# Six more places for first-stage weights, scale and shift in one run, and banks taken two by two

## The chip, the cores and the metric

The kernel runs on one core of one Trainium2 chip. Its time is device microseconds from launch to end, given as the median of several executions. Besides, one execution was profiled; durations and waits below are from that one. Its engines are called as in the profile: PE is TensorE, PEld its weight loads, DVE is VectorE, ACT ScalarE, POOL GpSimd, and SP SyncE, which issues most transfers.

## What is computed

Two layers on a stream of 256 tokens with 2048 channels, beside 256 tokens of context, all in 32-bit floats:

```python
shift, scale, gate = split(silu(c) @ ada_w[i] + ada_b[i], 3)
h  = rms_norm(x, norm_g[i]) * (1 + scale) + shift          # the same for ctx with c_ctx
# layer 0, heads side by side
p  = h @ w_in                     # query, gate, z, key, value, x, B, C, dt
ya = neighbourhood_attention(q, k, v, k_ctx, v_ctx, rpb) * silu(gate_a)
yb = gated_group_rmsnorm(bidirectional_ssd(conv(x, B, C), dt) + d * x, z)
x  = x + gate * (concat(ya, yb) @ w_out)
# layer 1
bg, cg, hv, g = split(h @ sc_in, 4)
x  = x + gate * ((silu(g) * bg * conv3(cg * hv)) @ sc_out)
```

Scale and shift of layer 0 are needed before anything else: 2 x 2048 columns of `ada_w[0]`, of 2048 rows each. They are wanted for two conditioning vectors, that of the latent tokens and that of the context.

## The kernel before

**Numbers in two parts.** Every wide product is split: a weight block of 128 x 1024 floats lands in a raw place, ScalarE casts it to the rounded type as its high part (L407), VectorE subtracts to get the low part (L414), and TensorE makes three products of high and low parts. There are `NW` = 3 places for high and low parts, taken in turn: block k goes to place k mod 3, and it may be split when fewer than three blocks are ahead of it that aren't used up (`splits_try`, L440; `used`, L463).

**Raw places.** The pool `free_r` has five raw places of 128 x 1024 floats. In the first stage four tiles that are needed later only (`PT0`, `PT1`, `xtm`, `yi`) are lent to it as `spare`, nine in all. SyncE loads blocks in the order of the list `loads` (`issue`, L359) whenever a place is free. When the list of the first stage is through, `later_loads` (L485) takes the lent places out of the pool.

**The order is written by a planner.** The program is straight-line. While it is emitted, `Plan` (L38) keeps a model of when each engine and each piece of a tile is ready, with costs written by hand, and with transfers at `RATE` bytes per ns. Tasks are generators; `pump` (L272) and `force` (L293) emit the next step of a task where the model says that its engine and its inputs are ready. On the chip each engine works its queue strictly in the order emitted, and semaphores hold it where an input isn't there. The model knows a tile in units of 128 columns (L55). The tables `small` and `const` come in two loads each, an early one and a late one (L341, L343; L514, L515).

**The first stage** covers layer 0's key, value and query of the first four heads, and B of the first group, for eight indices j of 256 channels each. Normalised tokens are transposed in four blocks of 128 tokens (two latent, two context). For each j, `ada_gen` (L692) computes scale and shift of its 256 channels: eight raw blocks, four for scale and four for shift (`part` 0 and 1), each against 128 x 32 columns of the conditioning vectors (`cpad`), then a copy by ScalarE (L714), two transposes by TensorE, a sum by VectorE (L722) and two or one small operations. With it, ScalarE and VectorE make the high and low parts of h (L744, L746, L750). Then TensorE does key and value for four token blocks, query for two, and B. Key and value accumulate over j in SBUF: each j's product goes to a bank of its own, and `part_gen` (L770) adds it to the sum (L776). Query and B stay in two banks each over all j. For j = 0 the token blocks come one after the other: the three weight blocks of key, value and query are held until the last token block is through, and then three calls of `used` give their places back (L886).

**The output projection of layer 0** (L1704) runs in three passes over the 16 pairs of `mix` blocks: the first pass makes two groups of 512 output columns, the others one. Each group has two banks for its two token blocks. The first pass comes behind the value projection of the last four heads, whose four banks are copied out by `v_gen` (L998).

## Time and profile before

| | |
|---|---|
| median of 3 runs | 1796.73 us (1795.94 to 1799.53) |
| profiled execution | 1797.29 us |
| its span | 1795.5 us |
| TensorE busy | 1765.5 us, 98% |
| its weight loads | 1490.7 us, 83% |
| VectorE, ScalarE busy | 1292.8 us, 72%; 786.9 us, 44% |
| transfers | 374.67 MB, mean 209 GB/s |
| granted clock | 1.00 |

The span runs from the first to the last instruction of the profiled execution; its time holds 1.8 us around it. In a row of a timeline stand start, duration, engine, line, operation, tiles, shape, the count of instructions that were merged, and in brackets the engine's idle time before it and what ended that. A row of a table of stretches has the stretch, its length, each engine's busy time with its instructions, the granted clock, the transfers' share and GB/s. A row of waits has who waited for what: us in total, times, and the longest.

Matmuls overlap in time on TensorE. So a busy share near 100% doesn't say that nothing is lost, and the distance from one start to the next says more than a duration.

### The profile page before, as it was taken

The numbers are of one execution on the slowest core, as the hardware profiler recorded it, in microseconds if no ns is written. First come the engines' busy times: TensorE is split into PE (matmuls) and PEld (weight loads), VectorE is DVE, ScalarE is ACT, GpSimd is POOL, SyncE is SP. The second block draws the span as 40 slices with busy tenths as digits, with TensorE's granted clock in tenths as the row PEclk, the third lists the DMA queues.
The fourth block names the chain that finished last, engine by engine and source line by source line (L and its number), as shares of the span: only waits on it lengthen the run. The fifth ranks groups of instructions, "written<-read, shape, count | busy, mean of one in ns | idle before, by whom it ended". The sixth has DMA issues, their size and how long they took to land. (4 is left out here: it accounts for less than half of the span.)

```text
span 1795.5 us, 26501 instructions
## 1 busy us (share of the span) xinstructions
PE 1765.5 (98%) x10039; PEld 1490.7 (83%) x10039; DVE 1292.8 (72%) x2073; ACT 786.9 (44%) x1386; POOL 32.5 (2%) x28
## 2 busy tenths in 40 slices
PE   6999999999999999999999999999999999999998
PEld 4677988879888889888888898788888888888887
DVE  5656787888676878676877688786667877565665
ACT  5323544455242445242435344555444444444442
POOL 0000100001000000000001000000000000000000
PEclk9999999999999999999999999999999999999999
DMA  9987744666746665745764567657766786666564
GB/s 359 339 285 239 225 143 125 204 183 200 235 127 202 211 185 175 232 139 173 218 200 134 165 185 247 202 186 268 274 222 225 249 265 222 185 185 187 186 213 150
DMA packets 222368, 374.67 MB, mean 209 GB/s; under 512 B 32432, under 2 KB 69136, under 8 KB 222240
## 3 DMA queue, kind: packets, MB, share of 16 engines
q1 hardware_dynamic: 214928, 366.38, 64.0%
q10 hardware_dynamic: 7312, 6.61, 1.1%
q8 instruction: 78, 1.28, 0.3%
q14 instruction: 50, 0.41, 0.1%
HBM read 367.52 MB, written 6.72 MB: 208 GB/s over the span
## 5 line engine op out<-in xcount | busy, mean ns | idle before, releaser
L407 ACT CAST wH<-raw 128x1024 fp32r<-128x1024 f32 (+1 forms) x439 | 457.8, 1044 | 687.3 <-PE bank L189 561.3
L414 DVE TENSOR_TENSOR wL<-raw,wH 128x1024 fp32r<-128x1024 f32 (+1 forms) x439 | 531.5, 1214 | 250.0 <-ACT wH L407 247.2
L189 PE MATMUL bank<-h,wH 128*128 128x512 f32 x1024 | 362.5, 399 | 1.4 <-DVE h L1669 0.9
L189 PE MATMUL bank<-hH,wH 128*128 128x256 f32 (+1 forms) x1040 | 343.3, 330 | 0.8 <-ACT wH L407 0.8
L189 PE MATMUL bank<-hL,wH 128*128 128x256 f32 (+1 forms) x1040 | 338.0, 325 | 0.0
L189 PE MATMUL bank<-hH,wL 128*128 128x256 f32 (+1 forms) x1024 | 330.8, 323 | 0.8 <-DVE wL L414 0.6
L189 PE MATMUL bank<-h,wL 128*128 128x256 f32 x1024 | 287.6, 281 | 0.0
L189 PE MATMUL bank<-wH,hH 128*128 128x512 f32 x640 | 257.1, 402 | 3.9 <-ACT hH L744 2.6
L189 PE MATMUL bank<-wL,hH 128*128 128x512 f32 x640 | 250.4, 392 | 0.0
L189 PE MATMUL bank<-wH,hL 128*128 128x512 f32 x640 | 249.8, 391 | 0.1
L804 DVE SCALAR_TENSOR_TENSOR acc<-raw,csil,acc 128x512 f32<-128x512 f32 x256 | 191.8, 749 | 63.2 <-DMA raw<-in_ada_w 54.3
L189 PEld LDWEIGHTS bank<-h,wH 128*128 128x128 f32 x1024 | 192.4, 188 | 50.4 <-issue 1.5
L189 PEld LDWEIGHTS bank<-hH,wH 128*128 128x128 f32 x1040 | 196.5, 189 | 18.6 <-ACT wH L407 1.3
L189 PEld LDWEIGHTS bank<-hL,wH 128*128 128x128 f32 x1040 | 196.8, 189 | 15.5
L189 PEld LDWEIGHTS bank<-hH,wL 128*128 128x128 f32 x1024 | 194.0, 189 | 18.3 <-DVE wL L414 1.6
L189 PEld LDWEIGHTS bank<-h,wL 128*128 128x128 f32 x1024 | 193.4, 189 | 0.0
L189 PE MATMUL bank<-wH,mix 128*128 128x512 f32 x512 | 163.1, 393 | 1.1 <-DVE Vt L998 1.1
L189 PEld LDWEIGHTS bank<-wH,hH 128*128 128x128 f32 x640 | 120.2, 188 | 33.8 <-issue 5.0
L189 PEld LDWEIGHTS bank<-wH,hL 128*128 128x128 f32 x640 | 120.2, 188 | 26.1 <-DVE hL L750 0.6
L189 PEld LDWEIGHTS bank<-wL,hH 128*128 128x128 f32 x640 | 120.2, 188 | 24.7 <-DVE wL L430 0.5
L189 PEld LDWEIGHTS bank<-wH,mix 128*128 128x128 f32 x512 | 96.1, 188 | 21.7 <-DVE Vt L998 1.6
L189 PE MATMUL bank<-wL,mix 128*128 128x512 f32 x256 | 100.0, 391 | 0.3 <-DVE wL L414 0.3
(262 smaller groups left out, 1764.0 us busy)
## 6 DMA issues: line engine op xcount, KB each, us to landing
raw<-in_w_in SPq DMA_DIRECT2D x208, 512.0 KB
raw<-in_ada_w SPq DMA_DIRECT2D x128, 512.0 KB
raw<-in_sc_in SPq DMA_DIRECT2D x128, 512.0 KB
raw<-in_w_out SPq DMA_DIRECT2D x64, 512.0 KB
raw<-in_ada SPq DMA_DIRECT2D x37, 512.0 KB
raw<-in_sc_out SPq DMA_DIRECT2D x32, 512.0 KB
tmp<-dram_csr SPq DMA_DIRECT2D x32, 256.0 KB
PT<-in_ada SPq DMA_DIRECT2D x14, 512.0 KB
```

The source lines that it names most:

```text
L189: E(T.matmul(o, l, r, start=start, stop=stop, skip_group_check=True))
L407: E(S.copy(H, v))
L414: E(V.tensor_tensor(out=Lo, in0=v, in1=H.bitcast(F32), op=ALU.subtract))
L804: E(V.scalar_tensor_tensor(out=acc, in0=v[:, j], scalar=csil[:, 2 * k + j:2 * k + j + 1], in1=acc, op0=ALU.mult, op1=ALU.add))
```

## The change

Five things are changed.

1. Six more raw places in the first stage: `KT`, `KL`, `QT` and `QL` (tiles for key and query, two places in each of the first two) are made as tiles of the first stage first, and as what they were only after it. The pool has fifteen.
2. For j from 2 on, `ada_gen` waits for all eight raw blocks and multiplies them in one run into one bank, scale in its first 256 columns and shift in the others; one copy, four transposes, one sum, and three small operations follow. For j = 0 and 1 it stays as it was.
3. High and low parts have a list of free places in the place of k mod 3. At j = 0, when query is through (before the third token block's products), query's place is given back.
4. The planner's `RATE` goes from 270 to 310, and it knows `small` and `const` in units of two columns.
5. The output projection takes two banks ahead of each group's first block, not all banks of a pass ahead of its first block.

```diff
-    RATE = 270.0
+    RATE = 310.0
...
-            return [(n, u) for u in range(lo // 128, hi // 128 + 1)]
+            g = 2 if n[:5] in ("small", "const") else 128
+            return [(n, u) for u in range(lo // g, hi // g + 1)]
...
-    KT, QT, Vt, gt = st([128, 4, 512], "KT", F32R), st([128, 4, 256], "QT", F32R), st([128, 4, 512], "Vt"), st([128, 4, 256], "gt")
-    KL, QL = st([128, 4, 512], "KL", F32R), st([128, 4, 256], "QL", F32R)
+    Vt, gt = st([128, 4, 512], "Vt"), st([128, 4, 256], "gt")
...
-    spare = [t.rearrange("p a b -> p (a b)") for t in (PT[0], PT[1], xtm, yi)]
+    spare = [t.rearrange("p a b -> p (a b)") for t in (PT[0], PT[1], xtm, yi)] + \
+        [st([128, 1024], n, name=f"first{n}") for n in ("QT", "QL")]
+    for n in ("KT", "KL"):
+        kt = st([128, 2, 1024], n, name=f"first{n}")
+        spare += [kt[:, 0], kt[:, 1]]
...
+    free_w, in_use = deque(range(NW)), deque()
+
+    def place():
+        in_use.append(free_w.popleft())
+        return in_use[-1]
...
     def split():
...
+        w = place()
...
-        H = WH[k % NW][:, :nb * n].rearrange("p (b c) -> p b c", b=nb)
-        Lo = WL[k % NW][:, :nb * n].rearrange("p (b c) -> p b c", b=nb)
+        H = WH[w][:, :nb * n].rearrange("p (b c) -> p b c", b=nb)
+        Lo = WL[w][:, :nb * n].rearrange("p (b c) -> p b c", b=nb)
...
-        while pos["split"] < pos["use"] + NW and pos["split"] in RAW:
+        while free_w and pos["split"] in RAW:
...
     def used():
         pos["use"] += 1
+        w = in_use.popleft()
+        if w is not None:
+            free_w.append(w)
         splits_try()
...
+            if j > 1:
+                ks = [("ada", j, part, q) for part in range(2) for q in range(4)]
+                yield when(lambda: all(k in RAW for k in ks))
+                yield W_("PE", *[RAW[k][1] for k in ks], nb=1)
+                ps = bank()
+                for _, _, part, q in ks:
+                    raw, v = RAW.pop(("ada", j, part, q))
+                    for g in range(4):
+                        mm(ps[32 * g:32 * g + 32, part * 256:part * 256 + 256], cpad[:, 4 * q + g, :], v[:, g, :],
+                           q == 0 and part == 0, q == 3)
+                    give_raw(raw)
+                    issue()
+                yield W_("ACT", ps)
+                Rt = tmp()
+                E(S.copy(Rt, ps))
+                yield W_("PE", Rt)
+                for b in range(4):
+                    turn(ps[:, b * 128:(b + 1) * 128], Rt[:, b * 128:(b + 1) * 128])
+                give(free_t, Rt)
+                yield W_("DVE", ps)
+                E(V.tensor_reduce(out=AS, in_=ps.rearrange("p (b g c) -> p b c g", b=4, c=32)[:, :, 0:2, :], axis=AX.X, op=ALU.add))
+                E(V.tensor_tensor(out=A0[:, k2, :], in0=AS[:, 0:2], in1=bc(bs1[:, k2]), op=ALU.add))
+                E(V.tensor_tensor(out=A0[:, k2, :], in0=A0[:, k2, :], in1=bc(g0[:, k2]), op=ALU.mult))
+                E(V.tensor_tensor(out=S0[:, k2, :], in0=AS[:, 2:4], in1=bc(P_("ab0")[:, k2]), op=ALU.add))
+                give(free_b, ps)
+            else:
...
             for t in range(2, 4):
                 force(lambda: ("h", j, t) in got, (urgent,))
+                if t == 2:
+                    free_w.append(in_use[2])
+                    in_use[2] = None
+                    splits_try()
...
     force(lambda: all(("part", 7, key, t) in got for key in "KV" for t in range(4)), (urgent,))
+    KT, QT, KL, QL = st([128, 4, 512], "KT", F32R), st([128, 4, 256], "QT", F32R), st([128, 4, 512], "KL", F32R), st([128, 4, 256], "QL", F32R)
...
     for ns in ((0, 512), (1024,), (1536,)):
-        pss = [banks(2) for n in ns]
+        pss = []
...
-            for ps in pss:
+            for k in range(len(ns)):
+                if ip == 0:
+                    pss.append(banks(2))
+                ps = pss[k]
                 chunk(2 * order[ip], "act", ps, ip == 0, ip == 15, lambda i: (mH[i][:, 0], mH[i][:, 1]))
```

More of the change, by code (lines that the diff above doesn't have):

```diff
@@ L396, in split @@
                 low_part()
-            W = WH[k % NW].rearrange("p (b c) -> p b c", b=nb)
+            W = WH[w].rearrange("p (b c) -> p b c", b=nb)
             E(S.copy(W[:, :, :64], v))
@@ L432, in rest @@
                 RAW.pop(0)
+                place()
                 HL[0] = (H, Lo)
@@ L689 @@
     S0 = st([128, KB, 2], "S0")
+    AS = st([128, 4, 2], "AS")
     g0 = P_("g0")
@@ L695, in ada_gen @@
             k2 = slice(2 * j, 2 * j + 2)
-            for part, dst in ((0, A0), (1, S0)):
-                ps = None
-                for q in range(4):
-                    key = ("ada", j, part, q)
-                    w_ = 2 if j == 0 else 4
-                    if q % w_ == 0:
-                        ks = [("ada", j, part, q + i) for i in range(w_)]
-                        yield when(lambda: all(k in RAW for k in ks))
-                        yield W_("PE", *[RAW[k][1] for k in ks], nb=0 if ps is not None else 1)
-                    if ps is None:
-                        ps = bank()
-                    raw, v = RAW.pop(key)
+            if j > 1:
[5 more added lines that the diff above has]
+                    raw, v = RAW.pop(("ada", j, part, q))
                     for g in range(4):
-                        mm(ps[32 * g:32 * g + 32, :256], cpad[:, 4 * q + g, :], v[:, g, :], q == 0, q == 3)
+                        mm(ps[32 * g:32 * g + 32, part * 256:part * 256 + 256], cpad[:, 4 * q + g, :], v[:, g, :],
+                           q == 0 and part == 0, q == 3)
                     give_raw(raw)
@@ L712, in ada_gen @@
                 yield W_("ACT", ps)
-                Rt = half()
-                E(S.copy(Rt, ps[:, :256]))
+                Rt = tmp()
+                E(S.copy(Rt, ps))
                 yield W_("PE", Rt)
-                for b in range(2):
-                    turn(ps[:, 256 + b * 128:384 + b * 128], Rt[:, b * 128:(b + 1) * 128])
-                give(free_h, Rt)
+                for b in range(4):
+                    turn(ps[:, b * 128:(b + 1) * 128], Rt[:, b * 128:(b + 1) * 128])
+                give(free_t, Rt)
@@ L720, in ada_gen @@
                 yield W_("DVE", ps)
-                p2 = dst[:, k2, :]
-                E(V.tensor_reduce(out=p2, in_=ps[:, 256:].rearrange("p (b g c) -> p b c g", b=2, c=32)[:, :, 0:2, :],
-                                  axis=AX.X, op=ALU.add))
-                if part == 0:
-                    E(V.tensor_tensor(out=dst[:, k2, :], in0=p2, in1=bc(bs1[:, k2]), op=ALU.add))
-                    E(V.tensor_tensor(out=dst[:, k2, :], in0=dst[:, k2, :], in1=bc(g0[:, k2]), op=ALU.mult))
-                else:
-                    E(V.tensor_tensor(out=dst[:, k2, :], in0=p2, in1=bc(P_("ab0")[:, k2]), op=ALU.add))
@@ L729, in ada_gen @@
-                give(free_b, ps)
+                E(V.tensor_reduce(out=AS, in_=ps.rearrange("p (b g c) -> p b c g", b=4, c=32)[:, :, 0:2, :], axis=AX.X, op=ALU.add))
+                E(V.tensor_tensor(out=A0[:, k2, :], in0=AS[:, 0:2], in1=bc(bs1[:, k2]), op=ALU.add))
+                E(V.tensor_tensor(out=A0[:, k2, :], in0=A0[:, k2, :], in1=bc(g0[:, k2]), op=ALU.mult))
+                E(V.tensor_tensor(out=S0[:, k2, :], in0=AS[:, 2:4], in1=bc(P_("ab0")[:, k2]), op=ALU.add))
+                give(free_b, ps)
+            else:
+                for part, dst in ((0, A0), (1, S0)):
+                    ps = None
+                    for q in range(4):
+                        key = ("ada", j, part, q)
+                        w_ = 4 if j else 2
+                        if q % w_ == 0:
+                            ks = [("ada", j, part, q + i) for i in range(w_)]
+                            yield when(lambda: all(k in RAW for k in ks))
+                            yield W_("PE", *[RAW[k][1] for k in ks], nb=0 if ps is not None else 1)
+                        if ps is None:
+                            ps = bank()
+                        raw, v = RAW.pop(key)
+                        for g in range(4):
+                            mm(ps[32 * g:32 * g + 32, :256], cpad[:, 4 * q + g, :], v[:, g, :], q == 0, q == 3)
+                        give_raw(raw)
+                        issue()
+                    yield W_("ACT", ps)
+                    Rt = half()
+                    E(S.copy(Rt, ps[:, :256]))
+                    yield W_("PE", Rt)
+                    for b in range(2):
+                        turn(ps[:, 256 + b * 128:384 + b * 128], Rt[:, b * 128:(b + 1) * 128])
+                    give(free_h, Rt)
+                    yield W_("DVE", ps)
+                    p2 = dst[:, k2, :]
+                    E(V.tensor_reduce(out=p2, in_=ps[:, 256:].rearrange("p (b g c) -> p b c g", b=2, c=32)[:, :, 0:2, :],
+                                      axis=AX.X, op=ALU.add))
+                    if part == 0:
+                        E(V.tensor_tensor(out=dst[:, k2, :], in0=p2, in1=bc(bs1[:, k2]), op=ALU.add))
+                        E(V.tensor_tensor(out=dst[:, k2, :], in0=dst[:, k2, :], in1=bc(g0[:, k2]), op=ALU.mult))
+                    else:
+                        E(V.tensor_tensor(out=dst[:, k2, :], in0=p2, in1=bc(P_("ab0")[:, k2]), op=ALU.add))
+                    give(free_b, ps)
```

## The prediction

> **What bounds the kernel now.** I read the page's busy shares first, then the stretches of the first 165 us, then what TensorE waited for in the first stage and after it.

> ```profile
> span 1795.5 us, 26501 instructions
> PE 1765.5 (98%) x10039; PEld 1490.7 (83%) x10039; DVE 1292.8 (72%) x2073; ACT 786.9 (44%) x1386; POOL 32.5 (2%) x28
> ```
> ```profile
> 0.00:20.00 20.00, 7.82 (x64) 5.34 (x64) 9.64 (x30) 9.99 (x23) 1.31 (x6) 1.00 0.91 333
> 20.00:40.00 20.00, 16.39 (x100) 11.00 (x104) 13.08 (x35) 13.72 (x31) 1.61 (x4) 1.00 1.05 395
> 40.00:60.00 20.00, 18.91 (x182) 12.87 (x178) 12.23 (x31) 9.43 (x22) 0.00 (x0) 1.00 0.94 338
> 60.00:165.00 105.00, 103.66 (x707) 75.34 (x700) 63.21 (x118) 34.38 (x55) 0.00 (x0) 1.00 0.86 305
> ```
> ```profile
> PE bank L189 <- ACT hH L744: 2.6, 2, 1.4
> PE bank L189 <- DVE sz L776: 1.0, 1, 1.0
> PE bank L189 <- ACT wH L407: 0.8, 1, 0.8
> PE bank L189 <- DVE gt L776: 0.3, 1, 0.3
> ```
> ```profile
> SPq L375 <- DVE wL L414: 48.0, 16, 6.0
> SPq L375 <- PE bank L189: 21.3, 19, 3.6
> ```

> TensorE is the bound: 1765.5 of 1795.5 us. Of the 30 us that it idles, 12.18 lie in the first 20 us, 3.61 in the next 20, 1.09 in the next and 1.34 in the rest of the first stage (each is the length of the stretch less its first number); some 12 us are left for the other 1630 us. The granted clock is 1.00 in every stretch. The waits name the causes between 24 and 170 us: activations, a weight cast, and banks that additions on VectorE (L776) give back. Not one of them names a weight transfer. The last fence is the transfer queue's side of the first 170 us: the loads of scale and shift (L375) stood 48.0 us for a place whose last reader was the subtraction of the low parts on VectorE, and 21.3 us for one that TensorE was reading. So places do limit the loads, but TensorE doesn't feel it. In the first 40 us, where TensorE does idle, the loads already run at 333 and 395 GB/s, and six more places can't make that stretch shorter.

> **The change part by part.** Time can only come out of TensorE's chain. Its pitch, from start to start, is seen where nothing is late:

> ```profile
> 97.90 0.39 PE L189 MATMUL bank<-hL,wH 128*128 128x512 f32 x1
> 98.13 0.39 PE L189 MATMUL bank<-hH,wL 128*128 128x512 f32 x1
> 98.45 0.64 PE L189 MATMUL bank<-PT,cpad 128*32 128x256 f32 x8
> ...
> 99.77 0.61 PE L189 MATMUL bank<-xtm,cpad 128*32 128x256 f32 x8
> 100.31 0.50 PE L189 MATMUL bank<-hH,wH 128*128 128x512 f32 x1
> 100.65 0.39 PE L189 MATMUL bank<-hL,wH 128*128 128x512 f32 x1
> ```

> The pitch is 0.23 us, though one matmul is shown as 0.39: starts count, durations overlap.

> *Scale and shift in one run.* These rows hold one run of four weight blocks: eight records a block, and 0.44 us a block (a third of 98.45 to 99.77). Entering costs 0.32 instead of 0.23 (98.13 to 98.45), leaving 0.54 instead of 0.44 (99.77 to 100.31), and the first matmul after it 0.34 instead of 0.23: 0.09 + 0.10 + 0.11 = 0.30 us a run. Before, every index j has two runs; after, j from 2 to 7 has one of eight blocks: 6 x 0.30 = 1.8 us less. The four transposes that follow in one go cost as much as two and two, as far as a row tells; ScalarE copies once instead of twice and VectorE has one small operation less, both under TensorE's cover. Bounds: 1.0 (a wait moves into one of the runs) to 2.4 (0.10 saved at each of six turns too). I take 1.8.

> *The query place given back early.* The block for B of j = 0 can be cast only after all three places of j = 0 are used up:

> ```profile
> 49.25 0.40 PE L189 MATMUL bank<-wL,hH 128*128 128x512 f32 x1
> 49.79 2.52 ACT L407 CAST wH<-raw 128x512 fp32r<-128x512 f32 x3
> 50.48 0.50 PE L189 MATMUL bank<-hH,wH 128*128 128x512 f32 x1 [0.83 <-ACT wH L407]
> 50.81 0.40 PE L189 MATMUL bank<-hL,wH 128*128 128x512 f32 x1
> 51.47 0.50 PE L189 MATMUL bank<-hH,wL 128*128 128x512 f32 x1 [0.26 <-DVE wL L414]
> 51.80 0.39 PE L189 MATMUL bank<-hH,wH 128*128 128x512 f32 x1
> ```

> Four pitches take 2.55 us (49.25 to 51.80) where 0.92 would do: 1.63 us. With the place free from the third row block on, the cast is emitted some 14 us earlier, behind which ScalarE and VectorE carry the last block's normalisation. That work then queues behind it: of the 2.52 us of the three casts this one, half as wide as the other two, is about a fifth, 0.5 us, and so much it can cost at the waits that come here:

> ```profile
> 33.47 0.38 PE L193 MATMUL bank<-const,xs 128*128 128x128 f32 x2
> 35.21 0.49 PE L189 MATMUL bank<-wH,hH 128*128 128x512 f32 x1 [1.36 <-ACT hH L744]
> 35.79 0.50 PE L189 MATMUL bank<-wH,hL 128*128 128x512 f32 x1
> ...
> 38.21 0.40 PE L189 MATMUL bank<-wL,hH 128*128 128x512 f32 x1
> 38.89 0.33 PE L193 MATMUL bank<-const,xs 128*128 128x128 f32 x1 [0.29 <-ACT xs L594]
> ```

> Bounds -0.5 to 1.6; I take 1.6, because both engines idle in that stretch (20 to 40 us: VectorE 13.08, ScalarE 13.72 of 20).

> *Six more places, RATE 310, and two columns as the grain for the small tables.* These make no instruction; they change the order that the planner writes. Before, a late load of the small tables makes its model hold back readers of their early columns, since 128 columns are one unit, and it lets loads arrive at 270 GB/s where the chip gives 333 to 395. With both mended, the normalisation of the third and fourth block can stand ahead of the weights' low parts. What can go are the waits just quoted: 1.4 us before 35.21 by the row itself, and beyond a pitch 0.35 before 35.79 and 0.45 before 38.89: 2.2 us. Bounds: all of it gained, or as much again lost, -2.2 to 2.2; I take half, 1.1, as the loads' order and rate up to here don't change. The other wait is for banks:

> ```profile
> 82.31 2.08 ACT L744 ACTIVATE hH<-xm,S,A 128x256 fp32r<-128x256 f32 x4 [0.23 <-DVE S L728]
> ...
> 85.57 0.40 PE L189 MATMUL bank<-wL,hH 128*128 128x512 f32 x1
> 86.96 0.51 PE L189 MATMUL bank<-wH,hH 128*128 128x512 f32 x1 [1.00 <-DVE sz L776]
> ```

> 1.39 less 0.23 is 1.16 us, and with the 0.3 us on gt that the waits name, 1.5 us. Blocks that are there earlier let this chain run ahead of the key rows. I take 0.5, bounds -1.5 to 1.5. In the other 1630 us the 12 idle us can be dealt anew by RATE; I take nothing, bounds -2 to 2. The four tiles that lend their places are first written after the stage, so no wait is added there.

> *Banks two by two.* The output projection's first pass takes four banks before its first matmul:

> ```profile
> 1139.76 0.40 PE L189 MATMUL bank<-wH,mix 128*128 128x512 f32 x1
> 1140.56 1.28 DVE L998 COPY Vt<-bank 128x512 f32<-128x512 f32 x2
> 1141.30 0.50 PE L189 MATMUL bank<-wH,mix 128*128 128x512 f32 x1 [1.14 <-DVE Vt L998]
> ```

> TensorE already has the first pair and runs its first block; 1141.30 less 1139.76 less a pitch is 1.3 us that it waits for the second pair. The new order asks for that pair one block later, which leaves the copy of V (L998) where the planner puts it, behind casts and mixes. Nothing in the chip's queues gets a bank sooner for certain. Half, 0.7; bounds -1 to 1.3.

> *Sum:* 1.8 + 1.6 + 1.1 + 0.5 + 0.7 = 5.7 us. The profiled execution took 1797.3 us, its span of 1795.5 and 1.8 around it, and is 0.6 over the median of the runs shown: 1797.3 - 5.7 = 1791.6 there, **1791 us** as a median. All unfavourable bounds together give 1797.3 - 1.0 + 0.5 + 2.2 + 1.5 + 2 + 1 = 1803.5, all favourable ones 1797.3 - (2.4 + 1.6 + 2.2 + 1.5 + 2 + 1.3) = 1786.3. They don't fall together: the root of the squares of the distances from the values taken is 2.6 us down and 5.2 us up, so 1788 to 1796 is the forecast's own range.

> [...] In 60 to 165 us weight loads fill 75.34 of 105 us, 72%, while TensorE looks 99% busy. A row of wide matmuls without a gap reaches 0.188 of each 0.23 us, 82%:

> ```profile
> L189 PEld LDWEIGHTS bank<-wH,hH 128*128 128x128 f32 x640 | 120.2, 188 | 33.8 <-issue 5.0
> ```

> Filled up to 82%, the stretch would give 105 x (1 - 72/82) = 12.8 us. [...] This trace doesn't bear it out in full, since the narrow products of scale and shift take 20.28 us of that stretch on TensorE with only 9.65 us of weight loading:

> ```profile
> 60.00:165.00 105.00, 20.28 (x340) 9.65 (x332) 0.00 (x0) 1.00 0.86 305
> ```

> Without them 65.69 of 84.7 us are left, 78%, and 84.7 x (1 - 78/82) = 4.1 us of headroom, much of it the runs' entries, counted above.

> **The rivals.** *Nothing to gain (0.25).* The places fill, TensorE never waited for them, and the planner gives the small gains back elsewhere. For it: the waits name no weight transfer. Then only the merged runs and part of the query place stay: 1.8 less about 1, so 1796.

> *More than that (0.10).* The blocks that lie ready let half of the 12.8 us close besides: 5.7 + 6.4 = 12.1 us, so 1785. Against it: the pitch of 0.23 between the runs.

> *Slower (0.14).* The one mechanism is the bank wait at 85.57. The merged run starts scale and shift together, and then four activations of 2.08 us; VectorE's subtractions wait for them in order, and the additions that give banks back queue behind. Of eight banks query and B hold four; two spare ones carry the key and value rows over two groups of six matmuls, 12 x 0.23 = 2.8 us. If the chain falls into the key rows at each of j = 1 to 7 and stands 2.08 us in front, 7 x 2.08 = 14.6 less the 1.5 of before is 13.1 us lost; with 5.2 gained elsewhere 7.9 more, 1805. It decides once the additions are over 2.8 us late more than twice. For it: two of seven already do. Against it: VectorE is busy 63.21 of 105 us.

> **How the numbers follow.** About 0.2%, 3.6 us, is what a measurement of this kernel can tell from no change: faster is under 1793.1, slower over 1800.3. The forecast has 0.51, of which 0.41 lie under 1793.1 and 0.10 within. More gain adds 0.10 and the first rival 0.05 to faster: 0.56. Same is 0.10 + 0.19 = 0.29 (the rest of the first rival, 0.01, is slower). Slower is 0.14 + 0.01 = 0.15. For eight in ten the range reaches from 1785.5 to 1801.

> **What would show it.** Right: in the profile after, one run of 64 narrow records for each j from 2; the cast of the B block of j = 0 before 40 us and no wait on L407 behind the last rows of j = 0; fewer loads held by L414; the wait on L998 at the head of the output projection gone or halved. The stage's gain of about 5 us should stand in the end undiminished, as every later stretch is TensorE's. Wrong: the L776 waits more than twice and longer than 1 us; a wait on L744 that is longer than before; idle time on TensorE in stretches after 205 us that grew by more than 2 us, which would be RATE; or idle time on a weight transfer, which would mean that 310 GB/s promises casts too early.

## The result, and the profile after

| | before | after |
|---|---|---|
| median | 1795.91 us (22 runs) | 1799.52 us (22 runs) |
| profiled execution, span | 1797.29 us, 1795.5 | 1799.83 us, 1797.9 |
| TensorE busy in it | 1765.5 us | 1766.0 us |
| mean granted clock in it | 1.00 | 0.997 |

The ratio is 1.0022, interval [1.0016, 1.0028]: slower, by 3.6 us, where 5 us less was forecast. The stretches of the first stage after (columns as before: stretch, length, busy time and instructions of PE, PEld, DVE, ACT, POOL, granted clock, DMA share, GB/s):

```profile
0.00:20.00 20.00, 7.77 (x68) 5.13 (x68) 9.58 (x30) 10.10 (x23) 1.32 (x6) 1.00 0.90 336
20.00:40.00 20.00, 16.14 (x85) 11.22 (x84) 13.22 (x36) 13.35 (x28) 1.61 (x4) 0.91 1.04 394
40.00:60.00 20.00, 19.99 (x150) 15.27 (x151) 13.07 (x30) 10.06 (x22) 0.00 (x0) 1.00 1.04 399
60.00:165.00 105.00, 102.65 (x742) 76.00 (x741) 64.64 (x120) 33.91 (x51) 0.00 (x0) 1.00 0.87 316
```

TensorE's idle time in them is 12.23, 3.86, 0.01 and 2.35 us (before 12.18, 3.61, 1.09 and 1.34): the third stretch won what the fourth lost. And the granted clock, 1.00 in every stretch of before, is 0.91 in the second. What TensorE waited for between 24 and 170 us, and then what it waited for behind 205 us, before, after, and in the fastest version found below (`...` stands for two rows, on x1b and on ScalarE's h, that are unchanged in the last fence; with them they count in the sums):

```profile
PE bank L193 <- ACT hH L788: 2.6, 2, 1.4
PE bank L193 <- DVE gt L820: 2.4, 2, 1.8
PE bank L197 <- ACT xs L609: 0.7, 1, 0.7
```
```profile
PE bank L189 <- DVE half L1435: 1.4, 2, 0.7
PE bank L189 <- DVE Vt L998: 1.1, 1, 1.1
PE bank L189 <- DVE h L1669: 0.9, 1, 0.9
PE bank L189 <- DVE wL L414: 0.7, 2, 0.4
...
PE bank L189 <- DVE tmp L1406: 0.6, 1, 0.6
...
```
```profile
PE bank L193 <- ACT Vt L1048: 2.1, 1, 2.1
PE bank L193 <- DVE half L1485: 1.7, 1, 1.7
PE bank L193 <- DVE tmp L1456: 1.1, 2, 0.7
PE bank L193 <- DVE wL L425: 0.9, 2, 0.7
PE bank L193 <- DVE h L1719: 0.9, 1, 0.9
...
```
```profile
PE bank L193 <- DVE h L1720: 0.9, 1, 0.9
PE bank L197 <- DVE x1b L1636: 0.6, 1, 0.6
PE bank L193 <- ACT h L1739: 0.6, 1, 0.6
```

Lines moved: L189 is L193 after, L193 is L197, L407 is L418, L414 is L425, L744 is L788, L776 is L820, L998 is L1048, L1406 is L1456, L1435 is L1485. Behind 205 us the named waits are 5.8 us before, 7.9 after, 2.1 in the fastest version. Two of them grew long, and after each comes something that the profile before does not have. Two of the timeline's stretches on TensorE (start, duration, operation; idle time before it in brackets), with the stretches around the first spell that follows:

```profile
404.14 0.39 PE L193 MATMUL bank<-wH,hL 128*128 128x512 f32 x1
406.26 0.61 PE L193 MATMUL bank<-const,half 128*128 128x1 f32 x4 [1.73 <-DVE half L1485]
...
408.28 0.63 PE L193 MATMUL bank<-wH,hL 128*128 128x512 f32 x1
408.70 0.63 PE L193 MATMUL bank<-wH,hH 128*128 128x512 f32 x1
...
1150.31 0.50 PE L193 MATMUL bank<-wH,mix 128*128 128x512 f32 x1 [2.05 <-ACT Vt L1048]
```
```profile
404.20:407.61 3.41, 1.68 (x10) 1.21 (x9) 2.26 (x7) 3.17 (x10) 0.00 (x0) 1.00 0.73 272
407.62:411.02 3.40, 3.40 (x10) 2.65 (x9) 2.64 (x7) 1.44 (x4) 0.70 (x1) 0.50 0.16 26
411.03:414.44 3.41, 3.41 (x29) 2.62 (x27) 2.29 (x4) 0.81 (x1) 0.00 (x0) 1.00 0.35 129
```

For 3.41 us behind the wait the clock is 0.50, and a wide matmul starts every 0.42 us (408.28 to 408.70) in place of 0.23. TensorE looks fully busy in that row, 3.40 of 3.40 us; only the clock column, or the pitch, tells. Half speed for 3.41 us loses 1.7 us (3.41 x 0.50, an estimate). The records of the clock after have three such spells up to the last matmul: from 25.32, 407.62 and 1151.72 us. In the profile before there is none. The first of the three has no long wait ahead of it, only two short ones:

```profile
22.42 0.44 PE L197 MATMUL bank<-const,half 128*128 128x128 f32 x2 [0.49 <-ACT half L758]
24.08 0.73 PE L193 MATMUL bank<-wH,hH 128*128 128x512 f32 x2 [1.22 <-ACT hH L788]
```

**An account of the two profiles.** I take each step from one matmul's start to the next, and as its normal length the median of such steps between the same two shapes over several profiles of both kernels, spells left out. After less before is then: normal lengths -2.5 us (fewer entries into runs of narrow products), the three spells +5.0, waits beyond the normal step +0.7 (-0.8 up to 200 us, +1.5 behind), small excesses and both ends -0.7; together +2.5, and the spans differ by 2.4. So in this pair the half-clock spells alone outweigh all that was won. Over all 22 runs after, the mean clocks amount to about two spells a run, over the sets of runs of before below to 0.5 to 1.0; at 1.7 us a spell that would be some 2 of the 3.6 us, an estimate.

### The profile page after: what moved, and what is told of

Read it like the earlier page. It is cut to its first block, busy times and chain, and to the rows that moved or that the text cites. A ratio compares the mean times of both kernels' runs of the same rounds, so it can differ in the third digit from the quotient of the medians.

```text
span 1797.9 us, 26441 instructions
## 1 busy us (share of the span) xinstructions
PE 1766.0 (98%) x10039; PEld 1493.6 (83%) x10039; DVE 1290.9 (72%) x2067; ACT 786.1 (44%) x1380; POOL 30.9 (2%) x28
## 3 DMA queue, kind: packets, MB, share of 16 engines
q8 instruction: 78, 1.28, 0.3%
## 5 line engine op out<-in xcount | busy, mean ns | idle before, releaser
L418 ACT CAST wH<-raw 128x1024 fp32r<-128x1024 f32 x427 | 447.8, 1049 | 671.6 <-PE bank L193 562.7
L425 DVE TENSOR_TENSOR wL<-raw,wH 128x1024 fp32r<-128x1024 f32 x427 | 519.7, 1220 | 241.4 <-ACT wH L418 234.7
L193 PE MATMUL bank<-h,wH 128*128 128x512 f32 x1024 | 356.0, 392 | 1.6 <-DVE h L1719 0.9
L193 PE MATMUL bank<-hH,wH 128*128 128x256 f32 (+1 forms) x1040 | 344.1, 331 | 0.0
L193 PE MATMUL bank<-hL,wH 128*128 128x256 f32 (+1 forms) x1040 | 338.7, 326 | 0.0
L193 PE MATMUL bank<-hH,wL 128*128 128x256 f32 (+1 forms) x1024 | 330.4, 323 | 0.0
L193 PE MATMUL bank<-h,wL 128*128 128x256 f32 x1024 | 287.0, 280 | 0.0
L193 PE MATMUL bank<-wH,hH 128*128 128x512 f32 x640 | 258.9, 405 | 4.9 <-ACT hH L788 2.6
L193 PE MATMUL bank<-wL,hH 128*128 128x512 f32 x640 | 252.7, 395 | 0.0
L193 PE MATMUL bank<-wH,hL 128*128 128x512 f32 x640 | 251.4, 393 | 0.1
L193 PEld LDWEIGHTS bank<-h,wH 128*128 128x128 f32 x1024 | 191.6, 187 | 44.6 <-issue 1.4
L193 PEld LDWEIGHTS bank<-hH,wH 128*128 128x128 f32 x1040 | 195.4, 188 | 19.1 <-issue 1.4
L193 PEld LDWEIGHTS bank<-hL,wH 128*128 128x128 f32 x1040 | 195.8, 188 | 16.2
L193 PEld LDWEIGHTS bank<-hH,wL 128*128 128x128 f32 x1024 | 193.1, 189 | 17.9
L193 PEld LDWEIGHTS bank<-h,wL 128*128 128x128 f32 x1024 | 193.5, 189 | 0.1
L193 PE MATMUL bank<-wH,mix 128*128 128x512 f32 x512 | 163.0, 395 | 2.1 <-ACT Vt L1048 2.1
L193 PEld LDWEIGHTS bank<-wH,hH 128*128 128x128 f32 x640 | 121.0, 189 | 34.1 <-issue 3.4
L193 PEld LDWEIGHTS bank<-wH,hL 128*128 128x128 f32 x640 | 121.0, 189 | 27.6 <-DVE hL L794 0.6
L193 PEld LDWEIGHTS bank<-wL,hH 128*128 128x128 f32 x640 | 121.0, 189 | 25.0 <-DVE wL L425 0.4
L193 PEld LDWEIGHTS bank<-wH,mix 128*128 128x128 f32 x512 | 96.8, 189 | 22.9 <-ACT Vt L1048 2.5
L193 PE MATMUL bank<-wL,mix 128*128 128x512 f32 x256 | 100.9, 394 | 0.9 <-DVE wL L425 0.9
```

Source lines behind the costliest of these rows:

```text
L193: E(T.matmul(o, l, r, start=start, stop=stop, skip_group_check=True))
L418: E(S.copy(H, v))
L425: E(V.tensor_tensor(out=Lo, in0=v, in1=H.bitcast(F32), op=ALU.subtract))
```

## The experiments

Each table compares with runs of before taken beside it on the same chip; `before` was 1794.99, 1795.55, 1796.0, 1795.81 and 1795.86 us in these five sets (15 to 29 runs each). Theory at first: the new order that `RATE` 310 and the late request for banks write makes waits behind the first stage, and the waits bring spells of half clock. Rival: the first stage itself gained less than its parts promise.

### RATE and banks undone, and stalls made on purpose

`a_rate270` is after with `RATE = 270.0`; `a_banks_first` is after with the old request for banks:

```diff
-        pss = []
+        pss = [banks(2) for n in ns]
...
-                if ip == 0:
-                    pss.append(banks(2))
```

`a_rate270_banks_first` undoes both.

> The changed kernel with RATE back at 270, all else kept. Theory 'idle spells that cost twice': the changed kernel's profile has three spells in which TensorE ran at half clock for 3.41 us (1.7 us lost each), and each comes right behind an idle spell of about 2 us; one of them is the wait for the sum of squares near 404 us (1.7 us idle), which the new order brought. Without RATE 310 that wait is 0.7 us again and its half-clock spell is gone: 1.0 + 1.7 = 2.7 us less, 1796.8. Rival 'the order as a whole': RATE 310 costs many small waits, and 270 gives 4 to 6 us back, 1794 to 1795.5. Rival 'the first stage costs it': no change, 1799 to 1800.

> The changed kernel with all four banks taken ahead of the output projection's first block again, all else kept. Theory 'idle spells that cost twice': the copies of V come earlier in the queues, the wait for the second pair goes from 2.1 us back to 1.1 and the half-clock spell behind it goes: 1.0 + 1.7 = 2.7 us less, 1796.8. Rival 'the first stage costs it': no change. Rival 'the order as a whole': 1.0 us less, 1798.5, with as many half-clock spells as before.

> The changed kernel with both undone, so the first stage's changes alone. Theory 'idle spells that cost twice': the first stage gained 3 us at full clock and keeps them, 1799.5 - 2.7 - 2.7 = 1794.1, about 2 us under the kernel before. Rival 'the first stage costs it': 1799, as the changed kernel.

| | median, runs | ratio to before |
|---|---|---|
| a_rate270 | 1797.04 us, 11 | 1.0012 [0.9999, 1.0024] |
| a_banks_first | 1799.98 us, 11 | 1.0024 [1.0015, 1.0032] |
| a_rate270_banks_first | 1797.85 us, 11 | 1.0016 [1.0007, 1.0025] |

Only the first came out near what was expected, and by luck: the mean clocks of its runs amount to 2.6 spells a run, more than after's, so the spells that were to go did not. With 270 throughout, the waits behind 205 us shrink, but the first stage's grow; of its waits between 24 and 205 us:

```profile
PE bank L193 <- ACT hH L788: 4.1, 3, 2.0
PE bank L193 <- DVE hL L794: 1.9, 1, 1.9
```

and a spell of twice the length, 6.83 us, follows at 57.8 us; another stands at 685.8 us. The banks asked for early changed nothing: the wait on L1048 stands there with 2.6 us, longer than after. The order of the copy and not that of the request made it.

`b_stalls` prices the spells. It is the kernel before, with 16 stalls in the third projection (it adds zeros to a bank, and writes 2, 4, 6 or 9 times zeros into a tile that the second zero product must wait for):

```diff
+                if kb == 6 and (i, part) in STALL:
+                    z = bias[0][:, 0, :]
+                    T.matmul(ps[0][:, :32], ident, z[:, :32], start=False, stop=False, ...)
+                    for _ in range(STALL[i, part]):
+                        G.memset(z, 0.0)
+                    T.matmul(ps[0][:, :32], ident, z[:, :32], start=False, stop=False, ...)
```

> The kernel before with sixteen stalls put into the third projection, 20 us or more apart: TensorE adds zeros to a bank, GpSimd sets a small tile 2, 4, 6 or 9 times, and TensorE adds zeros again and so waits for it. Four stalls of each length, about 0.9, 1.5, 2.0 and 2.9 us by GpSimd's 0.28 us a piece and 0.4 us around it. Theory 'idle spells that cost twice': the short ones cost their length, those of 2 us and more have a half-clock spell of 3.41 us behind them in most cases, the shortest never; time = before + about 29 us of stalls + 1.7 us for each half-clock spell, with 5 to 9 of these: 1833 to 1840. Rival 'the clock has another cause': no half-clock spells, 1825.

It took 1848.55 us (4 runs; 1.0297 [1.0279, 1.0314]), more than expected, since the stalls came out longer (0.79, 1.59, 2.33 and 3.43 us, some 0.4 us for each further set, where in before's row at 38.03 us two take 0.56; no run shows the 0.4 us that were allowed around them) and eleven spells came where 5 to 9 were expected. One of each of three lengths, a second one of 1.59 us, and the stretches of 3.4 us behind them:

```profile
1349.15 0.41 PE L1836 MATMUL bank<-bias,const 128*128 128x32 f32 x2 [0.79 <-POOL bias L1835]
...
1374.00 0.41 PE L1836 MATMUL bank<-bias,const 128*128 128x32 f32 x2 [1.59 <-POOL bias L1835]
...
1400.29 0.41 PE L1836 MATMUL bank<-bias,const 128*128 128x32 f32 x2 [2.33 <-POOL bias L1835]
...
1584.96 0.41 PE L1836 MATMUL bank<-bias,const 128*128 128x32 f32 x2 [1.59 <-POOL bias L1835]
```
```profile
1349.20:1352.60 3.40, 3.40 (x20) 2.99 (x21) 3.40 (x6) 1.36 (x2) 0.00 (x0) 1.00 0.31 75
1374.10:1377.50 3.40, 3.40 (x21) 3.01 (x22) 0.38 (x1) 0.31 (x1) 0.00 (x0) 1.00 0.88 307
1401.01:1404.40 3.39, 3.39 (x12) 2.91 (x12) 2.61 (x6) 0.00 (x0) 0.00 (x0) 0.50 0.84 285
...
1585.33:1588.70 3.37, 3.37 (x12) 2.89 (x12) 0.12 (x1) 0.00 (x0) 0.00 (x0) 0.50 0.60 184
```

Behind the 0.79 us idle the clock stays at 1.00, with 20 matmuls in 3.4 us; behind 2.33 us it is 0.50, with 12. 1.59 us stands between: no spell behind 1374.00, one in the last row, behind 1584.96. Of the 16 stalls, none of the four of 0.79 to 0.86 us had a spell behind it, three of the four of 1.59 to 1.93, and all eight of 2.33 and 3.43. The steps over the stalls, less a normal one each, sum to 34.8 us; eleven spells at 1.71 are 18.8; together 53.6, as much as the medians differ (the profiled execution itself lies 4.8 us over its median and has one more spell, at 25 us).

The spells start on a grid: 1401.00, 1428.31, 1479.51 and 1506.81 us lie 8, 15 and 8 times 3.413 us apart, and after's three, from 25.32 to 1151.72 us, 112 and 218 times. What halves the clock is not shown; what can be counted is how much TensorE idled between two lines of such a grid.

The grid tells the two stalls of 1.59 us apart. Counted from 1401.00, one of its lines lies at 1373.69 us and cuts the stall before 1374.00 into 1.29 and 0.30 us; the stall before 1584.96 lies whole between two lines, the second at 1585.32, where its spell starts. I laid such a grid over each of the twenty profiles, set by its own records of the clock, from 18 us to the last matmul, and summed TensorE's idle time in each stretch of 3.413 us: behind every stretch with 1.77 us or more the clock was halved, behind none with less than 1.55, and between these seven were followed by a spell and five were not. The two exceptions are stretches already at half clock, in `a_rate270` and `b_rate310`, where a spell lasted two of them, 6.83 us. In after the stretches ahead of its three spells hold 1.72, 1.73 and 2.00 us of idle time, and the next fullest, from 86.76 to 90.17 us, has 1.60 and no spell behind it; before's fullest, from 33.13 to 36.54 us, has 1.45. So here short waits added up between two lines (0.49 and 1.22 us ahead of after's spell at 25.32 us), and a wait that a line cut in two went free (after's 1.80 us ahead of 90.37, with a line at 90.18).

### Filling the gaps; the merged run undone

`a_fill` and `b_fill` put transposes and zero products that nobody reads in front of the places where TensorE waited, so that it isn't idle there: after, 12 before the first wide product, 12 before j = 0's key rows of the third token block, 16 before the sum of squares (L1485), 14 in j = 3, 8 at the second pair of the output projection; before, 12, 12, 8 and 4, none in j = 3. `a_two_runs` undoes the merged run; `b_again` is before, unchanged, for a second profile: it took 1795.04 us, and the excess over normal steps behind 205 us was 40.0 us in it, 42.6 in the first; so far do two executions of one kernel differ.

```diff
-            if j > 1:
+            if j > 99:
```

> The changed kernel with TensorE kept at work in its long idle spells by instructions that the planner doesn't see, so that the order is the same: 12 transposes ahead of the first product, 12 ahead of the third block's key rows, 16 ahead of the first group's sum of squares (404 us), and products with zeros added to a bank at 88 us (14) and ahead of the output projection's second pair (8). Theory 'idle spells that cost twice': the waits stay as long, but the half-clock spells behind them go: from about 2.1 a run (mean granted clock 0.9980) to under 1, clock 0.9992 or more, and 2 to 3 us less, 1797. Rival 'the waits themselves': the clock may rise, the time stays at 1799.5 or is up to 3 us longer by what the filling adds.

> The kernel before, filled at the same places (12, 12, 8 and 4). It has about 0.6 half-clock spells a run. Theory 'idle spells that cost twice': little to win, 0 to 1 us less, 1794 to 1795. So the filled changed kernel stands 2 to 3 us over it. Had the change kept the 3 us that its first stage gains in the profile, the filled changed kernel would be under this one: 1792.

> The changed kernel with scale and shift in two runs again for every j, all else kept. If the merged run saves what the two profiles' structure says, 6 times 0.3 to 0.45 us, this is 1.8 to 2.8 us slower than the changed kernel, 1801.3 to 1802.3. Rival 'the merged run brings the first stage's waits' (activations and bank additions late, as it needs eight blocks at once): 1 to 3 us faster, 1796.5 to 1798.5.

| | median, runs | ratio to before |
|---|---|---|
| a_fill | 1801.49 us, 5 | 1.0036 [1.0022, 1.005] |
| b_fill | 1794.34 us, 11 | 0.9997 [0.9988, 1.0006] |
| a_two_runs | 1799.36 us, 9 | 1.0025 [1.0015, 1.0035] |

Fillers are no remedy. They halved the spells, by the mean clocks from two a run to one, but the fillers took more time than that gave, and the waits moved. The merged run's undoing should have shown 1.8 us or more, and did not. Its profile shows why it cannot be read from the time: a wait of another place came up, 3.73 us,

```profile
213.75 0.38 PE L193 MATMUL bank<-hH,wL 128*128 128x256 f32 x1 [3.73 <-DVE wL L425]
```

with a spell from 214.4, while those at 25 us, 407 us and 1151 us went. These edits of the first stage let the planner write what follows differently. So the first stage and what lies behind it had to be taken apart.

### 270 behind the first stage only

```diff
     got.add(("V", 0))
+    plan.RATE = 270.0
```

`h_270later` is after with this line; `h_270later_banks_first` has the old request for banks besides. `b_rate310` is before with `RATE = 310.0` throughout and nothing else; `a_no_query` is after without the early return of the query's place.

> The changed kernel with RATE 310 in the first stage and 270 behind it, and the output projection's four banks taken ahead. By the profiles, TensorE's waits in the first 200 us are 33 us in the changed kernel but 39 us with RATE 270 throughout (activations of j = 1 late at 54 us); behind 200 us they are 35 us in the changed kernel, 34 in the kernel before, and 29 with RATE 270 and the banks ahead. Theory 'RATE 310 helps the first stage and hurts the rest': both good halves together, 1795.3 - 3.6 (first stage at full clock) and up to 5 behind it, 1787 to 1792. Rival 'each change redeals all later waits': the planner's state at the seam is another one, later waits anywhere in 29 to 36 us, 1789 to 1798.

> The same with banks two by two as in the changed kernel. Theory 'RATE 310 helps the first stage and hurts the rest': within 1.5 us of the one with the banks ahead, 1787 to 1793; if asking for the second pair later is what delays the copies of V, the wait at the output projection's head is over 2 us here and about 1 us there.

> The kernel before with RATE 310 alone. Theory 'RATE 310 hurts the rest': without the first stage's other changes it brings waits near 400 and 1150 us of 2 us with half-clock spells behind them, 1 to 1.5 spells more a run: 1797 to 1800. Rival 'each change redeals all later waits': 1793 to 1798, with the long waits at other places.

> The changed kernel without giving the query place back early. The wait for the cast and the subtraction behind the last rows of j = 0 comes back: 1.6 us more, 1801, and 3 more if a half-clock spell follows. Rival 'each change redeals all later waits': that wait is seen at 50 us, but the end is anywhere in 1796 to 1803.

| | median, runs | ratio to before |
|---|---|---|
| h_270later_banks_first | 1789.16 us, 5 | 0.9962 [0.995, 0.9974] |
| h_270later | 1791.16 us, 5 | 0.9967 [0.9954, 0.998] |
| b_rate310 | 1804.71 us, 6 | 1.0044 [1.003, 1.0057] |
| a_no_query | 1799.55 us, 12 | 1.0019 [1.001, 1.0027] |

One line turns the change from 3.6 us slower to 4.8 faster, and with the banks as before to 6.8 faster; no spell lies within the profile of the latter, one of `h_270later`'s at 91.07 us. The 4.8 us are not the first stage's: the 1683rd matmul, by which all these kernels have done the same products, starts at 274.76 us before and at 274.69 us in `h_270later` (that spell included), and what follows takes 1520.7 and 1515.7 us, though both have 270 there. Between the two requests for banks the intervals overlap, so there is no verdict on that part. `b_rate310` is worse than expected. Of its waits behind 205 us the first is

```profile
PE bank L189 <- DVE wL L414: 6.7, 2, 5.2
```

The undoing of the query's return left the total unmoved, too.

### Is a higher RATE harmful as such, and what are the parts worth in quiet

`b_310later` is before with 310 behind the first stage only; `h_290later`, `h_280later` and `h_260later` are `h_270later` with that number. `h_two_runs` and `h_no_query` are `h_270later` with one part undone.

> The kernel before, with RATE raised from 270 to 310 only behind the first stage (as soon as the first value block is through); the first stage stays as it was. If 310 is wrong for the later stages as such, its time is that of before plus what the change lost behind its first stage: after less the version with 270 behind the first stage, 1799.5 - 1791.2 = 8.3 us, half to all of it, so 1800 to 1804, with at least one half-clock spell behind 200 us. If each value of RATE only deals the waits anew, by luck, it can come out on either side of before, 1793 to 1799.

> The change with RATE 290 behind the first stage (310 in it), banks two by two. If a higher RATE there is harmful as such, the time lies between the version with 270 (1791.2) and the change (1799.5): 1793 to 1797. If each value only deals the waits anew, it can come out anywhere from 1789 to 1800, and under 1791 or over 1798 would speak for that.

> The change with 270 behind the first stage and the merged run undone, two runs for every j. If the merged run is worth what the prediction said and it shows once the later stages are quiet: 1791.2 + 1.8 to 4.0 = 1793 to 1795.2. If its gain goes into other waits of the first stage, as undoing it in the change suggested: 1791, within a microsecond.

> The change with 270 behind the first stage and without the early return of the query's place. If the wait at 49 us comes back (2.4 us in the change without the early return, and a half-clock spell of 3.41 us behind it, 1.7 us): 1791.2 + 1.6 to 4.1 = 1792.8 to 1795.3. If the wait is only moved: 1791, within a microsecond.

> The change with RATE 260 behind the first stage, banks two by two. The promise to the planner differs by 4% from the version with 270 (1791.2), so a smooth effect of RATE, with 8.3 us between 270 and 310, would move the time by 2 us at most: 1789 to 1791.5. If the order that any value writes is a draw of its own, it may come out anywhere from 1787 to 1800, with later waits of 38 to 50 us over the pitches, and 793.5 or more (1793.5) would show it.

> The change with RATE 280 behind the first stage, banks two by two. A smooth effect, between 270 (1791.2) and 290 (1798.2), gives 1793 to 1796.5. If each value is a draw of its own: anywhere from 1787 to 1800, and under 1791.5 or over 1798 would show it.

The last columns are the account by steps: what lies beyond the normal steps, spells included, up to 205 us and behind, in the profiled execution of each, which need not lie at the median (`h_280later`'s took 3.1 us less).

| | median, runs | ratio to before | to 205 us | behind |
|---|---|---|---|---|
| h_270later_banks_first | (above) | | 33.7 | 34.9 |
| h_260later | 1789.74 us, 5 | 0.9962 [0.995, 0.9975] | 34.2 | 35.7 |
| h_270later | (above) | | 34.9 | 37.4 |
| h_no_query | 1791.48 us, 7 | 0.9971 [0.996, 0.9982] | 35.0 | 35.7 |
| h_two_runs | 1792.41 us, 11 | 0.9984 [0.9975, 0.9992] | 32.4 | 37.0 |
| b_310later | 1793.22 us, 11 | 0.9986 [0.9977, 0.9995] | 31.9 | 37.9 |
| h_280later | 1795.09 us, 11 | 0.9995 [0.9986, 1.0004] | 33.9 | 37.7 |
| before | | | 32.0 | 42.6 |
| h_290later | 1798.23 us, 11 | 1.0009 [1.0, 1.0018] | 34.3 | 42.4 |
| after | | 1.0022 [1.0016, 1.0028] | 34.2 | 45.8 |
| a_no_query | (above) | | 36.5 | 46.4 |
| b_rate310 | (above) | | 38.7 | 47.8 |

Read the last column down: the order of the times is nearly the order of the excess behind 205 us, which runs from 34.9 to 47.8, while the excess in the first stage stays within 31.9 to 35.0 but for the two kernels at the end. These are single profiles, though: the two of before differ by 2.6 behind 205 us. With the first stage of the change the time grows with the later `RATE`, 1789.7, 1791.2, 1795.1, 1798.2, 1799.5 for 260 to 310: it rises at each step, though the value for 290 lies 0.2 us past the mark that had been set for luck, while those for 260 and 280 lie where a smooth effect put them. But before with 310 there became faster, by 2.6 us, against that theory. The longest sum among its waits behind 205 us is

```profile
PE bank L189 <- DVE wL L414: 1.5, 2, 0.8
```

where `b_rate310`, with the same later value, has 6.7 us there. So the value alone doesn't decide; it acts with the state in which the planner leaves the first stage. Why stays open.

The early return in quiet is told by these rows between 24 and 205 us of `h_no_query`:

```profile
PE bank L193 <- ACT wH L418: 2.2, 1, 2.2
PE bank L193 <- DVE sz L820: 0.6, 1, 0.6
PE bank L193 <- DVE gt L820: 0.6, 1, 0.6
```

Without it the wait on the cast is back, 2.2 us, but the waits on L820 are 1.2 us in place of after's 2.4 (`h_290later`, which has after's first stage, too has 2.4). In `h_270later` the wait on L820, 1.79 us between two lines of its grid, has the spell at 91.07 us behind it; `h_no_query` has none. The totals agree within their intervals. The merged run: 1792.41 against 1791.16 is 1.25 us, between what the two theories expected, with intervals that overlap; by normal steps the two profiles differ by 1.9 us.

## Why the prediction was wrong, point by point

**The step that failed** is "In the other 1630 us the 12 idle us can be dealt anew by RATE; I take nothing, bounds -2 to 2." By the 1683rd matmul, at 273 us, the profile after is 1.4 us ahead, where the first stage's terms promised 5.0; what follows takes 3.9 us more, where nothing was taken for the order and 0.7 less for the banks. So of the 8.2 us by which the sum missed the profile 4.6 lie behind and 3.6 ahead; the points below go through the latter. Between the change and the change with 270 there lie 8.4 us in the medians (1799.52 and 1791.16), and the one line edits nothing in the first stage. So this term, with 0 taken, was +3.9 in after and, by the count above, -5.0 in `h_270later`. That the latter stands at the 1791 of the forecast is luck: it won its time where nothing was forecast. The sign that the prediction itself named, over 2 us more idle time behind 205 us, all but came: the named waits grew by 2.1, the idle time up to 1790 us by 1.7. Two things made the bound too narrow. The planner writes another order for the whole rest, not for a few waits; and an idle spell was priced at its own length. The second is the smaller part: of the 8.9 us by which the two profiles differ behind the 1683rd matmul, after's two spells are 3.4. Why the order for 310 has the longer waits is not shown.

**The granted clock.** "The granted clock is 1.00 in every stretch" was true and was carried over to a kernel not seen. Behind the stretches in which after's TensorE idled 1.72 to 2.00 us, 1.7 us more went each time (the estimate above), and before's rows already held two of the waits: 0.7 on L1435 became 1.7, 1.1 on L998 became 2.1.

**Scale and shift in one run: right.** After, j = 4's run reads

```profile
95.11 0.40 PE L193 MATMUL bank<-hH,wL 128*128 128x512 f32 x1
95.44 1.93 PE L193 MATMUL bank<-raw,cpad 128*32 128x256 f32 x32
...
98.48 0.61 PE L193 MATMUL bank<-yi,cpad 128*32 128x256 f32 x8
99.03 0.50 PE L193 MATMUL bank<-hH,wH 128*128 128x512 f32 x1
99.36 0.40 PE L193 MATMUL bank<-hL,wH 128*128 128x512 f32 x1
```

64 narrow records: 4.25 us from 95.11 to 99.36, of which eight blocks of 0.434 (95.44 to 98.48, seven blocks) are 3.47 and two wide pitches 0.46; 0.32 remain, once where there were two. Six of them are 1.9 us, 1.8 was taken.

**The query's place: right where it was looked for, not in the sum.** The B block of j = 0 is cast at 36.76 us, and behind the third row block TensorE runs on:

```profile
36.76 0.61 ACT L418 CAST wH<-firstKT 128x512 fp32r<-128x512 f32 x1
```
```profile
50.40 0.39 PE L193 MATMUL bank<-wL,hH 128*128 128x512 f32 x1
50.63 0.39 PE L193 MATMUL bank<-hH,wH 128*128 128x512 f32 x1
```

1.6 us went, but "-0.5 to 1.6; I take 1.6" left out that TensorE, let through, meets the next late chain sooner.

**The bank wait (L820)** is that chain. 0.5 less was taken; the "wrong" sign was more than two waits of over 1 us, and the waits stayed two, but the longer one grew:

```profile
88.17 0.40 PE L193 MATMUL bank<-wL,hH 128*128 128x512 f32 x1
90.37 0.51 PE L193 MATMUL bank<-wH,hH 128*128 128x512 f32 x1 [1.80 <-DVE gt L820]
```

2.20 less a pitch is 1.97, where 1.16 was. The rival that was built on it, 13 us, did not come, as two waits are not seven.

**The activations' waits**, 1.1 less: nothing. The wait on L788 stands at 35.91 us with 1.36 us, to the digit as before. So the first stage as a whole gave far less than 5: the 1683rd matmul starts at 273.35 us in place of 274.76, 1.4 us ahead with one spell of 1.7 within. Fewer loads stood for a place that the low parts' subtraction was reading, as the signs of "right" had it (60.7 us up to 170 us before, L375 and L377; 40.8 after, L379 and L381), and TensorE got nothing from it. No version takes back the six places or the grain of two columns alone, so what each does by itself stays open.

**Banks two by two**, 0.7 less: the wait on the second pair went from 1.14 to 2.05 us and then bore a spell. The copy came late; on ScalarE a weight cast stands right ahead of it:

```profile
1148.75 1.03 ACT L418 CAST wH<-raw 128x1024 fp32r<-128x1024 f32 x1
1149.68 1.06 ACT L1048 COPY Vt<-bank 128x512 f32<-128x512 f32 x2
```

As `a_banks_first` has the same wait, and `h_270later` with the late request names none there, the request isn't its cause.

**The weight loads' share of the stretch from 60 to 165 us** was rightly not taken for 12.8 us to be won: it gave nothing, the weight loads went from 75.34 to 76.00 us of 105.

## What to carry to other kernels

Where a planner writes the order of straight-line code, a changed cost that reaches past the stage it was meant for is a change to the whole kernel, and its effect there can have either sign (8.4 us lost here, 2.6 won in `b_310later`): confine it to that stage, and measure the two parts apart. Look for the longest waits on TensorE before predicting, and where one could grow as long as those that had a spell behind them here, price it with the spell: in after, stretches of 3.41 us with 1.72 us of idle time or more lost some 1.7 us besides (the estimate above), one with 1.60 had no spell. An edit's gain in one place is not seen in the total when the place behind it is late as well: read it from the steps in the profile, not from the time alone.
